# Layer 0's FFN: two groups of a modulation's rows in one PSUM bank, turned once, and both streams' gates turned together

## The chip, the cores and the metric

The kernel runs on one core of one Trainium2 chip. The metric is device time in microseconds (us) of one execution. Engines are named as in the profile: PE is TensorE's matmul pipe and PEld its weight load, DVE is VectorE, ACT is ScalarE, POOL is GpSimd, and SPq is the queue on which SyncE issues DMAs. L252 is line 252 of the kernel before.

## What is computed

Two transformer layers over 512 latent rows and 256 context rows (the two *streams*), 1024 columns wide. Every sub-layer is normed, scaled, shifted and gated by vectors that come from a conditioning vector of its stream:

```python
s_c = jax.nn.silu(c)
s_cc = jax.nn.silu(c_ctx)[None, :]
for l in range(DEPTH):
    mx = (s_c @ mod_w[l] + mod_b[l])[:, None, :]
    mc = (s_cc @ mod_w[l] + mod_b[l])[:, None, :]
    shx1, scx1, gx1, shx2, scx2, gx2 = jnp.split(mx, 6, axis=-1)
    shc1, scc1, gc1, shc2, scc2, gc2 = jnp.split(mc, 6, axis=-1)
    hx = _rms(x, norm_mix_w[l]) * (1.0 + scx1) + shx1
    ...
    x = x + gx1 * ax
    x = x + gx2 * _swiglu(_rms(x, norm_ffn_w[l]) * (1.0 + scx2) + shx2, ffn_w_in[l], ffn_w_out[l])
```

So a layer has six *modulations* (parts 0 to 5), each a product of a vector with 1024 rows by 1024 columns of `mod_w`. Parts 2 and 5 are the gates. Layer 1's parts 2 to 5 are needed for the latent stream alone.

## The kernel before

The work is written out in one order: layer 0's attention with its projections (to about 340 us in the profile), layer 0's FFN in two stages, gate/up products (about 428 to 764 us) and the way out (764 to 950 us), then layer 1 in the same manner. From early in layer 0's attention on, PE runs its instructions in the order in which the code is written (a manual schedule for PE). For DVE, ACT, POOL and the DMA queues a scheduler that works with modelled times picks the order, so a small edit can reorder them at some distance.

The gate/up stage is a list of matmul blocks (`product`, L933) for 22 slices f of the hidden width. Its operands come in as 128x512 pieces (`wr`), are split by ACT into a high part (`wbh`, L901) and by DVE or POOL into a low part (`wbl`, L911); ACT and DVE also add up the partial products (L938 to L973). In the list of blocks a hook stands twice per f from f = 2 on, 40 times in all. Each call of the hook makes one step of a stream of modulation work (`mod_stream`), so that the vectors that are needed later are made in the shade of the FFN's matmuls.

`mod_stream` takes a list of *groups* of 256-column *chunks*. A chunk is loaded as two pieces of 128 x 4 x 256 (L211). `products` multiplies them by the conditioning vectors and adds the eight row blocks, on DVE (L224, L226) for one stream and on ACT and POOL (L230 to L236) for the other; what is left is one accumulator `ma` of 128 x 256 per chunk and stream whose 128 rows are still to be summed. When all chunks of a group are through, `sums` runs, in two steps of the hook:

- step one: for each of the group's four accumulators one matmul with 32 columns of ones (L245) writes the column sums, 32 times over, into one quarter (32 partitions) of a PSUM tile `modrow`, and ACT copies it back to SBUF (L248);
- step two: two matmuls (L252) with a selection matrix from the constants turn these rows into columns, `modcol`, in the same PSUM bank, and DVE adds the bias, a chunk at a time (`add_mod`, L276), into `modc`; for parts 1 and 4 it also makes the scale `aff` (L280).

In the gate/up stage the groups are (layer, part) = (0, 5), (1, 0), (1, 1), for both streams, with two chunks in a group and so two groups for each of the three, and (1, 2) for the latent stream alone, with four chunks in one group: seven groups. All of them use the PSUM bank `acc1`, which nothing else uses there. In the way out three more groups follow, parts 3, 4 and 5 of layer 1, one stream and four chunks each.

A gate is multiplied with rows of tokens, so it is needed as a row on all partitions. `gate_mem` (L285) turns one stream's gate from 128 x 8 to 8 x 128 with one matmul (L288), copies it out of PSUM (L290, tile `grow`, two buffers) and stores it to DRAM (L292, `gmem`); `gate_row` (L294) later reads it back to all 128 partitions (L300, tile `g`, 512 KB). It is called twice at the end of the second head group of layer 0's attention (L1326), and through a list `gates` by the three hooks that follow the stream's end; `gate_mem(1, 5, 0)` comes in layer 1.

Transposes use two PSUM banks, `tr0` and `tr1`. `tr_tile` (L102) hands them out by turns, unless the caller names one. The attention of layer 0 names them for `ppt`, the transposed probabilities: even blocks go to `tr0` and are copied out by ACT (L617), odd blocks to `tr1` and are copied out by DVE (L615). The transposes of q and k (`qpt`, L535, and `kpt`, L543, copied out by ACT at L537 and L544) and a gate's (`gps`) take the banks by turns.

The way out (`way_out0`, L1001) makes two passes over f, three row tiles each, with PSUM sums in six banks. For each f it loads 512 KB of `ffn_w_out` (`wdr`, L1016) and the hidden rows (`hidm`, L1014), splits both (L998 on ACT, L999 on DVE) and issues 18 matmuls (L1030 to L1032). Its first act is to read the two gates (0, 5) back; they are first used at the end of the first pass (L471). It keeps the last two f of a pass back to finish bank by bank.

Of the kernel before, what the change touches and what calls it, by code (L numbers as in the profile page):

```python
# [19 lines left out]
P = 128  # L20
# [19 lines left out]

C_ID, C_S2, C_ONE, C_S4 = 0, 128, 130, 258
C_N = C_S4 + 12

# [20 lines left out]
def backbone(es: ExitStack, tc: tile.TileContext, x, c, ctx, c_ctx, mod_w, mod_b, norm_mix_w, norm_ffn_w,  # L64
# [133 lines left out]
    def mod_stream(groups, pool, bank):  # L198

        width = 256  # L200
        pieces = [(g, c, pc) for g in groups for c in g for pc in range(2)]
        accs, raws, full, rows = {}, [], [], []

# [36 lines left out]
        def sums(g):  # L240
            every = [acc for c in g for acc in accs.pop(c)]
            m = len(every)
            ps = bank_tile("modrow", [P, width])
            for j, acc in enumerate(every):
                nc.tensor.matmul(ps[32 * j:32 * j + 32, :], cst[:, C_ONE:C_ONE + 32], acc, start=True, stop=True,  # L245
                                 tile_position=(0, 32 * j))
            r = every[-1]
            nc.scalar.copy(r[:32 * m], ps[:32 * m])  # L248
            yield
            ps = bank_tile("modcol", [P, 2, m])  # L250
            for b in range(2):
                nc.tensor.matmul(ps[:, b, :], r[:32 * m, b * P:(b + 1) * P], cst[:32 * m, C_S4:C_S4 + m],  # L252
                                 start=True, stop=True)
            i = 0
            for l, part, n, streams in g:
                add_mod(l, part, 2 * n, 2 * n + 2, ps[:, :, i:i + streams], streams)
                i += streams

        while pieces or raws or full or rows:
            if rows:  # L260
                for _ in rows.pop():
                    pass
            if full:
                rows.append(sums(full.pop()))
                next(rows[0])
# [18 lines left out]

    def gate_mem(l, part, i, bank=None):  # L285

        ps = tr_tile("gps", [KT, P]) if bank is None else p_1.tile([KT, P], F32, name="gps", tag=bank)
        nc.tensor.transpose(ps, modc[l][:, part, :, i], ident)  # L288
        row = small.tile([KT, P], F32, name="grow", tag="grow", bufs=2)
        nc.vector.tensor_copy(row, ps)  # L290
        mem = gmem[l, part, i] = dram.tile([KT, P], F32, name="gmem", tag=f"gmem{l}{part}{i}")
        nc.sync.dma_start(mem, row)  # L292

    def gate_row(l, part, i, pool):  # L294

        if (l, part, i) not in gmem:
            gate_mem(l, part, i)
        g = pool.tile([P, D], F32, name=f"g{i}", tag=f"g{i}")
        with tc.issue_after(turn["load"].ins):
            nc.sync.dma_start(g, dram_rows(gmem[l, part, i].rearrange("k p -> (k p)")))  # L300
        return g
# [988 lines left out]
    if True:  # L1290
        for i, (b, t) in enumerate(steps):
# [11 lines left out]
            if b < 3:  # L1303
# [188 lines left out]

    gates = [(0, 5, 0), (0, 5, 1), (1, 2, 0)]

# [114 lines left out]
    if True:  # L1609
# [34 lines left out]
        xs0, xs1 = xs, [None] * NTX  # L1644
        gate_mem(1, 5, 0)
        o_t = [keep.tile([P, D], F32, name=f"o{t}", tag="xo", bufs=6) for t in range(NTX)]
# [230 lines left out]
def _constants():  # L1877
# [53 lines left out]
```

## Time and profile before

| what | value |
|---|---|
| runs | 1691.99, 1696.72, 1697.31 us; median 1696.72 us |
| span of the profiled execution | 1695.6 us, 1.1 us below the median of the runs |
| PE busy over the span | 1631.5 us (96%) |
| DVE, ACT, POOL busy | 1146.7, 937.0, 696.4 us |
| gate/up stage of layer 0 | 428 to 763.6 us |
| matmuls of `modrow` (L245) and `modcol` (L252), all ten groups | 80 and 40 records, two for each matmul of the code |
| matmuls of `gps` (L288) | 6 |

The profile is one execution. Busy times overlap between engines. A timeline row gives the start in the span, the length from the first start to the last end of the merged instructions, how many there are, and, in brackets, how long the engine stood idle just before and what ended that. Matmuls overlap with the next one, so what one costs is read from start to start and not from its length. A windows row gives the busy time of each engine in a stretch, the clock that PE was granted, the share of the time that the DMA engines were busy, and GB/s.

### The profile page before, as it was taken

What the parts mean: (1) busy time and instruction counts of PE and PEld (TensorE: products, weight loads), DVE (VectorE), ACT (ScalarE), POOL (GpSimd) and SP (SyncE); (2) the same over time, 40 slices, a digit from 0 to 9 for tenths busy, and PEclk for the clock granted to TensorE, in tenths of its full rate; (3) what the DMA queues carried; (4) which work ended last, traced back from release to release, by engine and by line L of the source; (5) the groups of instructions that cost most, each with busy time, mean ns of one, the idle gap of its engine ahead of it and who ended that gap; (6) DMA issues with size and microseconds to landing.
All of it is one profiled execution on the core that took longest, in us unless ns stands there. A gap on an engine that the chain in (4) does not pass through costs nothing. (4 is left out here: it accounts for less than half of the span.)

```text
span 1695.6 us, 28585 instructions
## 1 busy us (share of the span) xinstructions
PE 1631.5 (96%) x10390; PEld 1468.6 (87%) x10390; DVE 1146.7 (68%) x2014; ACT 937.0 (55%) x2011; POOL 696.4 (41%) x867
## 2 busy tenths in 40 slices
PE   6999999899999999999999989999999999999998
PEld 3977787677999999998777889999988899999887
DVE  3765656754799887767767656666666598887434
ACT  5565555745456665545554456666666555555320
POOL 2665554321346554412413366666664242221000
PEclk8999999999999999999999999999999999999999
DMA  9222221411455555439966311111112433331431
GB/s 319 69 71 74 70 70 50 164 60 38 129 167 172 164 159 162 134 108 347 296 184 189 99 43 38 48 42 44 50 45 97 125 93 102 111 101 57 137 99 62
DMA packets 218108, 194.64 MB, mean 115 GB/s; under 512 B 20016, under 2 KB 202864, under 8 KB 217968
## 3 DMA queue, kind: packets, MB, share of 16 engines
q1 hardware_dynamic: 217616, 192.62, 36.8%
q8 instruction: 81, 1.33, 0.3%
q14 instruction: 59, 0.48, 0.1%
q10 hardware_dynamic: 352, 0.21, 0.0%
HBM read 179.92 MB, written 12.87 MB: 114 GB/s over the span
## 5 line engine op out<-in xcount | busy, mean ns | idle before, releaser
L901 ACT CAST wbh<-wr 128x512 fp32r<-128x512 f32 x170 | 104.9, 621 | 130.2 <-PE p L933 73.4
L933 PE MATMUL p<-hT,wbh 128*128 128x256 f32 (+1 forms) x752 | 154.5, 299 | 0.0
L465 PE MATMUL inps<-wih,hT 128*128 128x384 f32 x512 | 144.2, 344 | 7.3 <-ACT qkv L677 7.3
L911 POOL TENSOR_TENSOR wbl<-wr,wbh 128x512 fp32r<-128x512 f32 x43 | 60.0, 1396 | 173.6 <-ACT wbh L901 173.6
L933 PEld LDWEIGHTS p<-hT,wbh 128*128 128x128 f32 x752 | 121.9, 191 | 0.2
L911 DVE TENSOR_TENSOR wbl<-wr,wbh 128x512 fp32r<-128x512 f32 x127 | 107.7, 858 | 21.0 <-ACT wbh L901 16.8
L933 PE MATMUL p<-hT,wbl 128*128 128x256 f32 (+1 forms) x376 | 111.9, 298 | 0.0
L933 PE MATMUL p<-t,wbh 128*128 128x384 f32 (+1 forms) x480 | 111.3, 318 | 0.0
L604 POOL TENSOR_SCALAR Pt<-Pt,rc 128x256 f32<-128x256 f32 (+3 forms) x96 | 74.6, 788 | 89.3 <-DVE rc L601 83.1
L231 POOL TENSOR_TENSOR modp<-modp 128x512 f32<-128x512 f32 x40 | 57.4, 1436 | 114.3 <-ACT modp L230 114.3
L465 PEld LDWEIGHTS inps<-wih,hT 128*128 128x128 f32 x512 | 93.3, 188 | 10.6 <-ACT qkv L677 9.7
L933 PE MATMUL p<-hTt,wbh 128*128 128x256 f32 (+1 forms) x480 | 101.0, 302 | 0.0
L887 POOL TENSOR_TENSOR wr<-wr 128x512 f32<-128x512 f32 x40 | 61.6, 1540 | 89.8 <-DVE ws L892 85.8
L933 PE MATMUL p<-b,wbh 128*128 128x384 f32 x368 | 93.8, 336 | 0.2 <-DVE c L961 0.2
L901 ACT CAST wbh<-ws 128x512 fp32r<-128x512 f32 x120 | 69.4, 579 | 43.1 <-PE p L933 29.0
L224 DVE SCALAR_TENSOR_TENSOR ma<-modw,cols,ma 128x256 f32<-128x256 f32 x140 | 89.2, 637 | 2.3
L592 ACT ACTIVATE Pt<-sc,nm 128x256 f32<-128x256 f32 (+3 forms) x96 | 67.6, 707 | 35.3 <-DVE nm L588 16.9
L465 PE MATMUL inps<-wil,hT 128*128 128x384 f32 x256 | 86.0, 336 | 0.0
L933 PEld LDWEIGHTS p<-t,wbh 128*128 128x128 f32 x480 | 82.9, 189 | 0.0
L911 DVE TENSOR_TENSOR wbl<-ws,wbh 128x512 fp32r<-128x512 f32 x120 | 81.7, 681 | 1.7 <-ACT wbh L901 1.6
L933 PEld LDWEIGHTS p<-hTt,wbh 128*128 128x128 f32 x480 | 78.3, 191 | 3.1 <-ACT modp L230 1.6
L230 ACT ACTIVATE modp<-modw,cols 128x256 f32<-128x256 f32 x160 | 68.4, 500 | 18.0 <-POOL ma L236 10.1
(355 smaller groups left out, 5217.9 us busy)
## 6 DMA issues: line engine op xcount, KB each, us to landing
modw<-in_mod_w_dram SPq DMA_DIRECT2D x96, 512.0 KB, 5.2
wr<-in_ffn_w_in_dram SPq DMA_DIRECT2D x176, 256.0 KB, 2.9
wdr<-in_ffn_w_out_dram SPq DMA_DIRECT2D x66, 512.0 KB, 3.7
wir<-in_od_w_in_dram SPq DMA_DIRECT2D x96, 128.0 KB, 2.3
hidm<-hid SPq DMA_DIRECT2D x44, 192.0 KB, 1.9
hr<-hidm SPq DMA_DIRECT2D x22, 192.0 KB, 3.5
x<-in_x_dram SPq DMA_DIRECT2D x8, 512.0 KB, 3.5
wir<-in_ev_w_in_dram SPq DMA_DIRECT2D x16, 256.0 KB, 3.5
```

Of the source, the lines that this page charges most:

```text
L224: nc.vector.scalar_tensor_tensor(acc, w[:, k], scale[k], acc, ALU.mult, ALU.add)
L230: nc.scalar.activation(pr[:, k], w[:, k], AF.Copy, scale=scale[k])
L231: nc.gpsimd.tensor_add(pr[:, 0:2], pr[:, 0:2], pr[:, 2:4])
L465: nc.tensor.matmul(ps, hs[j][:, k, :], ws[k // 2][z][:, k % 2, c0:c1], start=(k, j, z) == (0, 0, 0), stop=(k, j, z) == (KT - 1, 1, 0))
L592: turn["exp"] = nc.scalar.activation(p[:, :n], s, AF.Exp, bias=nm[:, c1], accum_out=sm[:, c1])
L604: nc.gpsimd.tensor_scalar(p[:, :n], p[:, :n], rc[:, hh:hh + 1], 1.0, ALU.mult, ALU.mult)
L887: nc.gpsimd.tensor_sub(w, raw[f, "G1"], w)
L901: nc.scalar.copy(hi, w)
L911: (nc.gpsimd if name == "G2" else nc.vector).tensor_sub(lo, raw[need[n]], f32(hi))
L933: nc.tensor.matmul(ps, w[:, k, :], H[b][h][:, k, :], start=first and k == 0 and q == 0, stop=final and k == 3 and q == 2, skip_group_check ...
```

## The change

For a modulation of both streams the two groups now share one `modrow` tile. The first group's four matmuls start the sums with a stationary matrix of 16 columns of ones and 16 of zeros; the second group's four add to the same bank with 16 of zeros and 16 of ones. So each quarter of the bank holds two rows' sums, 16 times each. Only after the second group ACT copies the bank, and two matmuls turn all eight rows at once, with a selection matrix of eight columns; DVE then adds the bias for all eight column blocks of both streams in one operation. Groups of one stream use ones throughout as before, and their four chunks also get one bias operation instead of four. `modcol` is now 128 x 8 x streams, and the matmul for each half of a chunk writes every second column block of it.

`gate_mem` takes the number of streams: with two it turns both gates in one matmul of 16 columns, copies 16 rows and stores them with one DMA, interleaved by column block. Read back, one stream's gate is then eight pieces of 512 bytes in DRAM, where it was one run of 4 KB. `grow` has one buffer. The constants have 48 more columns.

```diff
-C_ID, C_S2, C_ONE, C_S4 = 0, 128, 130, 258
-C_N = C_S4 + 12
+C_ID, C_S2, C_ONE, C_S4, C_S8 = 0, 128, 146, 290, 298
+C_N = C_S8 + 20
...
-            m = len(every)
-            ps = bank_tile("modrow", [P, width])
+            l, part, n, streams = g[0]
+            ends = 2 * (n + len(g)) == KT
+            if not n:
+                rowed.append(bank_tile("modrow", [P, width]))
+            ps = rowed[0]
+            one = C_ONE if not n and ends else C_ONE + P - 16 if not n else C_ONE - 16
             for j, acc in enumerate(every):
-                nc.tensor.matmul(ps[32 * j:32 * j + 32, :], cst[:, C_ONE:C_ONE + 32], acc, start=True, stop=True,
+                nc.tensor.matmul(ps[32 * j:32 * j + 32, :], cst[:, one:one + 32], acc, start=not n, stop=ends,
                                  tile_position=(0, 32 * j))
+            if not ends:
+                return
             r = every[-1]
-            nc.scalar.copy(r[:32 * m], ps[:32 * m])
+            nc.scalar.copy(r, rowed.pop())
             yield
-            ps = bank_tile("modcol", [P, 2, m])
+            ps = bank_tile("modcol", [P, KT, streams])
             for b in range(2):
-                nc.tensor.matmul(ps[:, b, :], r[:32 * m, b * P:(b + 1) * P], cst[:32 * m, C_S4:C_S4 + m],
+                nc.tensor.matmul(ps[:, b::2, :], r[:, b * P:(b + 1) * P], cst[:, C_S4:C_S4 + 4 * streams],
                                  start=True, stop=True)
-            i = 0
-            for l, part, n, streams in g:
-                add_mod(l, part, 2 * n, 2 * n + 2, ps[:, :, i:i + streams], streams)
-                i += streams
+            add_mod(l, part, 0, KT, ps, streams)
...
-    def gate_mem(l, part, i, bank=None):
+    def gate_mem(l, part, streams, bank=None):
...
-        nc.tensor.transpose(ps, modc[l][:, part, :, i], ident)
-        row = small.tile([KT, P], F32, name="grow", tag="grow", bufs=2)
+        nc.tensor.transpose(ps, cs, ident)
+        row = small.tile([2 * KT, P], F32, name="grow", tag="grow", bufs=1)[:KT * streams]
         nc.vector.tensor_copy(row, ps)
-        mem = gmem[l, part, i] = dram.tile([KT, P], F32, name="gmem", tag=f"gmem{l}{part}{i}")
-        nc.sync.dma_start(mem, row)
+        mem = dram.tile([KT, streams, P], F32, name="gmem", tag=f"gmem{l}{part}")
+        gmem.update({(l, part, i): mem[:, i, :] for i in range(streams)})
+        nc.sync.dma_start(mem.rearrange("k i p -> (k i) p"), row)
...
-            nc.sync.dma_start(g, dram_rows(gmem[l, part, i].rearrange("k p -> (k p)")))
+            nc.sync.dma_start(g.rearrange("p (k c) -> p k c", c=P), dram_rows(gmem[l, part, i]))
...
-                    for k in range(2):
-                        gate_mem(0, 2, k)
+                    gate_mem(0, 2, 2)
...
-    gates = [(0, 5, 0), (0, 5, 1), (1, 2, 0)]
+    gates = [(0, 5, 2), (1, 2, 1)]
...
-    k[:, C_S4:C_S4 + 4] = p[:, None] == 32 * np.arange(4)
+    k[:, C_S4:C_S4 + 8] = p[:, None] == 32 * (np.arange(8) % 4) + 16 * (np.arange(8) // 4)
```

How the order of instructions moves is shown at three places. The first is PE in the gate/up stage, one hook after the first group of (0, 5). `p` are the blocks' sums, `t`, `hT` and `wbh`, `wbl` their operands. Before:

```order
L933 MATMUL p_5741<-t_4884,wbh 128x384
L933 MATMUL p_5741<-t_4883,wbl 128x384
L252 MATMUL modcol<-cst,ma 128x4 x2
L933 MATMUL p_5929<-hT_110,wbh 128x384
L933 MATMUL p_5929<-hT_111,wbh 128x384
```

With the change, at the same place:

```order
L939 MATMUL p_5735<-t_4878,wbh 128x384
L939 MATMUL p_5735<-t_4877,wbl 128x384
L939 MATMUL p_5917<-hT_110,wbh 128x384
L939 MATMUL p_5917<-hT_111,wbh 128x384
L939 MATMUL p_5917<-hT_110,wbl 128x384
```

The pair of turning matmuls is gone here, and at two more such places; after the second group of each modulation it stands as `128x4x2 x2`. The rest of PE's order in the stage is the same, and so is the place of every `modrow`.

The second place is DVE in the same stage, one hook after the second group of (1, 1). `cg`, `c` are FFN partial sums. Before:

```order
L961 TENSOR_TENSOR c_7722<-p_7568,s_7600 128x384
L276 TENSOR_TENSOR modc_107<-modcol,bcol 128x4 x2
L911 TENSOR_TENSOR wbl<-ws,wbh 128x512
L280 SCALAR_TENSOR_TENSOR aff_109<-modc_107,cols 128x4 x2
L892 TENSOR_TENSOR ws<-wr 128x512
```

With the change:

```order
L967 TENSOR_TENSOR c_7691<-p_7538,s_7570 128x384
L279 TENSOR_TENSOR modc_107<-modcol,bcol 128x16
L917 TENSOR_TENSOR wbl<-ws,wbh 128x512
L283 SCALAR_TENSOR_TENSOR aff_109<-modc_107,cols 128x16
L898 TENSOR_TENSOR ws<-wr 128x512
```

Two small operations become one wider one, and at the first group of a modulation none is left. Over the whole kernel DVE issues 29 operations fewer, ACT 3, PE 8, and SPq 2.

The third place is PE in layer 0's attention, where the gates (0, 2) are turned. `sc` are scores, `mod` the attention's own modulation work. Before:

```order
L182 MATMUL mod<-modw,s_pad 32x256 x8
L191 MATMUL modcol<-cst,modr 128x2 x2
L288 MATMUL gps<-cst,modc_106 8x128 x2
L578 MATMUL sc<-kT,qt 128x256 x2
L612 MATMUL ppt<-cst,Pt 128x128 x8
```

With the change:

```order
L182 MATMUL mod<-modw,s_pad 32x256 x8
L191 MATMUL modcol<-cst,modr 128x2 x2
L293 MATMUL gps<-cst,modc_106 16x128
L584 MATMUL sc<-kT,qt 128x256 x2
L618 MATMUL ppt<-cst,Pt 128x128 x8
```

One `gps` instead of two takes one transpose bank instead of two. From here to the end of layer 0's attention `qpt` takes `tr0` and `kpt` takes `tr1`, where it was the other way round; ACT's and DVE's orders differ in some places of this stretch, mostly by one or two positions.

More of the change, by code (lines that the diff above doesn't have):

```diff
@@ L201, in mod_stream @@
         pieces = [(g, c, pc) for g in groups for c in g for pc in range(2)]
-        accs, raws, full, rows = {}, [], [], []
+        accs, raws, full, rows, rowed = {}, [], [], [], []
         def bank_tile(name, shape):
@@ L264, in mod_stream @@
                 rows.append(sums(full.pop()))
-                next(rows[0])
+                next(rows[0], None)
             if len(raws) == 2 or not pieces and raws:
@@ L1644, in backbone @@
         xs0, xs1 = xs, [None] * NTX
-        gate_mem(1, 5, 0)
+        gate_mem(1, 5, 1)
         o_t = [keep.tile([P, D], F32, name=f"o{t}", tag="xo", bufs=6) for t in range(NTX)]
```

7 lines of the change are left out of this document (5 added, 2 removed).

## The prediction

> **What bounds the kernel now.** I read the page first, then busy time by stretch for the places that the change touches.
>
> ```profile
> span 1695.6 us, 28585 instructions
> PE 1631.5 (96%) x10390; PEld 1468.6 (87%) x10390; DVE 1146.7 (68%) x2014; ACT 937.0 (55%) x2011; POOL 696.4 (41%) x867
> ...
> GB/s 319 69 71 74 70 70 50 164 60 38 129 167 172 164 159 162 134 108 347 296 184 189 99 43 38 48 42 44 50 45 97 125 93 102 111 101 57 137 99 62
> ```
>
> PE is busy for 96% of the span. By stretch (layer 0's attention after the gates are turned; one stretch inside it; then the gate/up stage; then the first pass of the way out and its end):
>
> ```profile
> core 0: us, PE busy (x) PEld busy (x) DVE busy (x) ACT busy (x) POOL busy (x), PEclk, DMA share, GB/s
> 221.00:335.00 114.00, 105.57 (x782) 83.05 (x782) 72.82 (x134) 71.95 (x160) 49.95 (x69) 1.00 0.31 104
> 310.00:315.00 5.00, 4.45 (x44) 3.52 (x43) 2.25 (x5) 3.15 (x6) 0.55 (x1) 1.00 0.99 375
> ...
> 500.00:550.00 50.00, 50.00 (x300) 48.67 (x298) 47.65 (x78) 29.57 (x64) 29.29 (x25) 1.00 0.60 180
> 700.00:750.00 50.00, 50.00 (x295) 49.16 (x294) 30.54 (x52) 25.67 (x48) 14.96 (x12) 1.00 0.24 72
> 765.00:840.00 75.00, 75.00 (x339) 61.60 (x338) 59.12 (x85) 42.29 (x77) 29.60 (x24) 1.00 0.99 327
> 840.00:850.00 10.00, 8.33 (x36) 6.32 (x35) 3.70 (x4) 5.04 (x8) 2.27 (x3) 0.99 0.79 266
> ```
>
> In the gate/up stage PE has no gap: 50.00 of 50 us at full clock. DVE is next with 47.65 of 50, but nothing on PE waits for it. So in this stage a matmul taken out of PE's order shortens the span by its slot, and operations taken from DVE and ACT bring nothing. In the attention PE stands idle for 114 - 105.57 = 8.4 us, so order and waits matter there. The way out's first pass is full on two sides: PE 75.00 of 75, DMA 0.99.
>
> **The turns that go.** PE's timeline at one of them:
>
> ```profile
> 549.08 0.51 PE L933 MATMUL p<-t,wbh 128*128 128x384 f32 x2
> 549.42 0.34 PE L933 MATMUL p<-t,wbl 128*128 128x384 f32 x1
> 549.60 0.50 PE L252 MATMUL modcol<-cst,ma 128*128 128x4 f32 x4
> 549.96 0.59 PE L933 MATMUL p<-hT,wbh 128*128 128x384 f32 x2
> 550.39 0.34 PE L933 MATMUL p<-hT,wbl 128*128 128x384 f32 x1
> ```
>
> From wbl to the next start are 549.60 - 549.42 = 0.18 us. Without the turn the next wbl would start where a block's third matmul does, 0.34 us after 549.60 (549.08 to 549.42); it starts at 550.39. The turn holds PE for 0.79 - 0.34 = 0.45 us. Three go: **-1.3 us**. The sums (`modrow`) keep their count, shape and place; adding to a bank instead of starting it is assumed to cost nothing, as the FFN's own blocks do it throughout.
>
> The wait behind: the second group's sums now need no released bank, since the first left it open, and nothing else uses `acc1`. ACT's copy and the turn come one hook apart, as before. On the other engines go three ACT copies and, in the stage, 15 small DVE operations:
>
> ```profile
> L276 DVE TENSOR_TENSOR modc<-modcol,bcol x48: 142/152/163, 14.0 to 939.4; 128x4 f32<-128x4 f32 x32, 128x2 f32<-128x2 f32 x16
> ```
>
> At 0.15 us that is 2.3 us of DVE, under PE's cover: zero.
>
> **The gates.** One gate's turn in the stage:
>
> ```profile
> 737.39 0.34 PE L933 MATMUL p<-b,wbl 128*128 128x384 f32 x1
> 737.57 0.27 PE L288 MATMUL gps<-cst,modc 128*8 128x128 f32 x1
> 737.60 0.61 PE L933 MATMUL p<-hTt,wbh 128*128 128x384 f32 x2
> 738.04 0.34 PE L933 MATMUL p<-hTt,wbl 128*128 128x384 f32 x1
> ```
>
> 738.04 - 737.57 - 0.34 = 0.13 us; one of three goes: **-0.1 us**. Sixteen stationary columns should load like eight. With one buffer for `grow`, the second gate's copy waits for the first row's store, but the hooks are several us apart: zero.
>
> **The attention after the gates.** One `gps` goes there too, and with it a bank turn, so `qpt` and `kpt` swap banks against `ppt`'s fixed ones. The places where PE's waits hang on that:
>
> ```profile
> 221.64 1.07 PE L612 MATMUL ppt<-cst,Pt 128*128 128x128 f32 x8 [0.31 <-DVE grow L290]
> ...
> 225.23 0.63 PE L612 MATMUL ppt<-cst,Pt 128*128 128x128 f32 x4
> 226.60 0.66 PE L612 MATMUL ppt<-cst,Pt 128*128 128x128 f32 x4 [0.73 <-ACT qt L537]
> ...
> 267.28 1.09 PE L612 MATMUL ppt<-cst,Pt 128*128 128x128 f32 x8 [0.69 <-ACT kT L544]
> ...
> 292.12 0.66 PE L612 MATMUL ppt<-cst,Pt 128*128 128x128 f32 x4 [0.21 <-ACT qt L537]
> ...
> 295.06 1.09 PE L612 MATMUL ppt<-cst,Pt 128*128 128x128 f32 x8 [0.46 <-ACT kT L544]
> ```
>
> Before, `qpt` was in `tr1`, so the first four `ppt` ran and the second four waited for ACT's copy of q. Swapped, the first four wait too, and the second four follow them: about one half block, 0.4 us, later at 225 and at 292. Where `kpt` was in `tr0` (267, 295) it is the reverse, some 0.4 us earlier. These four cancel. The wait for `grow` at 221.64 can go, since the one `gps` now sits in `tr1`, and a `gps` slot goes (0.1): between 0 and -0.4 us, and I take **-0.2**. If all five waits went, it would be -(0.31 + 0.73 + 0.69 + 0.21 + 0.46) = -2.4 us. The other bound is +3, from the longest wait of `ppt` on a copy of q in the half of the attention before, which DVE's and ACT's new order could bring here as well:
>
> ```profile
> PE ppt L612 <- ACT qt L537: 3.1, 2, 2.9
> ```
>
> **The gates' way back.** Each read of a two-stream gate becomes 8 x 128 pieces of 512 bytes instead of 128 of 4 KB. The nearest rows are loads in pieces of 512 bytes (`wr`) and of 4 KB (`wdr`), and the gates' own:
>
> ```profile
> wr<-in_ffn_w_in_dram SPq DMA_DIRECT2D x176, 256.0 KB, 2.9
> wdr<-in_ffn_w_out_dram SPq DMA_DIRECT2D x66, 512.0 KB, 3.7
> ...
> g<-gmem SPq DMA_DIRECT2D x6, 512.0 KB, 8.0
> ```
>
> By throughput: the DMA engines move 180 / 0.60 = 300 GB/s of full share at 500 to 550 us, where the loads are `wr` and 1 KB pieces, and 375 / 0.99 = 379 at 310 to 315, where they are mostly 4 KB. 512 KB (0.524 MB) take 1.75 and 1.38 us, so two gates cost 0.7 us more. In the attention (reads at 312, first use at 341) that has cover. In the way out the reads stand in the queue at 765 us, in front of loads that keep the DMA engines at 0.99, and the pass ends on such loads:
>
> ```profile
> 765.35 0.90 SPq L300 DMA_DIRECT2D g<-gmem  x2
> ...
> 843.21 1.05 ACT L998 CAST hT<-wdr 128x1024 fp32r<-128x1024 f32 x1 [4.14 <-DMA wdr<-in_ffn_w_out_dram]
> ...
> 847.96 0.50 PE L1030 MATMUL dps<-hT,hTt 128*128 128x512 f32 x1 [0.61 <-ACT hT L998]
> ...
> 849.53 0.60 PE L1031 MATMUL dps<-hT,hTt 128*128 128x512 f32 x1 [1.06 <-DVE hT L999]
> ```
>
> PE loses 1.67 us there to loads that come late, so up to 0.7 can pass through; bounds 0 and +0.7, and I take **+0.4**, the middle. The Trainium skill, "DMA: Bandwidth & Descriptors", section Specifications, puts the least transfer for line rate at 512 bytes; by that rule this term would be zero and the sum 0.4 lower. The 300 against 379 GB/s above speak for a small cost.
>
> **The rest.** The constants are 48 x 512 bytes = 25 KB longer at a start that loads at 319 GB/s: **+0.1**. Two stores of 4 KB become one of 8 KB, twice: zero.
>
> Sum: -1.3 - 0.1 - 0.2 + 0.4 + 0.1 = -1.1 us, a span of 1694.5. The profiled span lies 1.1 us below the median of the runs, 1696.72, so the time is **1695.6 us**, 0.07% less. A measurement of this kernel can tell about 0.3% from no change, that is 5.1 us: the runs before themselves lie 5.3 us apart.
>
> **The rivals.**
> *Given back at the pass's end.* If the first pass hangs on its loads alone, PE comes to them earlier and waits longer, and only the attention's share and the start are left: 1696.6. For it speak the 0.99 and the 4.14 us wait on `wdr`; against it, that the loads start when PE frees their places, so they move ahead with PE.
> *Strided sums.* `modcol` is now written with gaps: for two streams eight bytes, for one stream four, then as many left out. No row of before shows a matmul that writes so. If it doubled a turn's slot of 0.45, seven turns remain (three and one in the stage, three in the way out): +3.2, 1698.8. Against it: a turn writes four or eight columns. The Trainium skill, "PSUM — Partial Sum Buffer", section Specifications (TRN2), says that a non-contiguous access pattern slows matmuls significantly, by cachelines of 8 bytes; this rival is what it would do here.
> *Slower: the gate reads hold up the way out.* If the small pieces cost by number and a gate took 16 us instead of 8.0, both would push 16 us of queue before the loads of a pass that has 0.75 us of free DMA time until 840 and 2.1 in the last 10 us. PE would wait some 13 us longer at the end: about 1708.5. It decides from 9 us of added queue time on. Against it: `wr` lands 256 KB of such pieces in 2.9 us.
> *Much faster: the attention's new order.* If ACT's and DVE's changed order took away half of PE's 8.4 idle us there, -4.2 with the -1.4 of the stage: 1691.1. For it: ACT's copies of `ppt` move ahead of other work; against it: PE's order is fixed and four of the five waits only change places.
> That the turns don't go is no rival, since the order shows them gone.
>
> **How the numbers follow.** The forecast 0.60; given back 0.15; strided sums 0.10; held-up way out 0.07; the attention's order 0.08. The last is the only one below 1691.6 (faster by over 0.3%), the one before it the only one above 1701.8, so faster 0.08, same 0.85, slower 0.07. The range, 1691.5 to 1699.0, takes in the first three cases, the attention's lower bound of -2.4 and most of its upper one.
>
> **What would show it.** Right: the `modcol` matmuls of the stage and the way out are 28 records instead of 40 at about 0.25 us, and a turn still holds PE for 0.45; the first way-out matmul starts 1.4 us earlier against the stage's start, with PE still at 50.00 of 50; ACT's copies of `modrow` are seven; PE's idle time from 221 to 335 us is 8.4 within 2; at the first pass's end PE waits 1.7 to 2.4 us. Wrong: longer `modcol` records (strided sums), gates that land after 12 us or more and a longer wait at the first pass's end (held up), or idle time in the attention that moves by over 3 us. A gap of PE inside the gate/up stage would undo the first term.

## The result and the profile after

The changed kernel takes 1699.37 us (median of 11 runs, 1695.48 to 1704.98), the kernel before beside it 1696.21 us (11 runs). The ratio is 1.0024, 95% interval 1.0015 to 1.0034: slower by some 4 us, where 1.1 us less was forecast and the range ended at 1699.0. The profiled execution of the changed kernel is the slowest of its eleven, 1704.98 us, so the spans are compared place by place, not as wholes. Of its page:

```profile
span 1703.2 us, 28521 instructions
PE 1641.3 (96%) x10376; PEld 1476.8 (87%) x10376; DVE 1148.5 (67%) x1985; ACT 935.9 (55%) x2008; POOL 698.7 (41%) x867
```

PE has 14 matmul records fewer (10390 before) and is busy 9.8 us longer (1631.5 before). First what the change was made of. One turn in the gate/up stage, in PE's timeline, and the records of the turns and of ACT's copies by tile:

```profile
552.32 0.34 PE L939 MATMUL p<-t,wbl 128*128 128x384 f32 x1
552.49 0.51 PE L258 MATMUL modcol<-cst,ma 128*128 128x8 f32 x4
552.85 0.60 PE L939 MATMUL p<-hT,wbh 128*128 128x384 f32 x2
553.29 0.34 PE L939 MATMUL p<-hT,wbl 128*128 128x384 f32 x1
```

```profile
L258 PE MATMUL modcol<-cst,ma x28: 167/253/257, 552.5 to 945.3; 128*128 128x4 f32 x16, 128*128 128x8 f32 x12
```

```profile
L254 ACT COPY ma<-modrow x7: 364/372/373, 544.2 to 941.5; 128x256 f32<-128x256 f32 x7
```

A turn holds PE for 553.29 - 552.49 - 0.34 = 0.46 us, there are 28 records and seven copies: all as forecast, and writing with gaps costs nothing here (median 253 ns, as before). Now the places, by busy time in stretches (layer 0's attention, the gate/up stage, the first pass of the way out, its end):

```profile
221.00:335.00 114.00, 105.58 (x801) 83.32 (x799) 72.12 (x134) 71.29 (x160) 52.94 (x71) 1.00 0.32 105
765.00:840.00 75.00, 74.71 (x339) 61.70 (x339) 56.41 (x82) 39.47 (x71) 26.05 (x22) 1.00 0.97 320
840.00:850.00 10.00, 10.00 (x46) 8.29 (x45) 5.08 (x6) 4.22 (x9) 4.47 (x4) 1.00 0.94 317
850.00:860.00 10.00, 6.89 (x17) 4.36 (x16) 6.22 (x7) 5.45 (x10) 2.78 (x2) 0.69 0.63 183
860.00:870.00 10.00, 9.80 (x42) 7.69 (x42) 8.16 (x12) 6.06 (x8) 1.79 (x5) 0.96 0.63 202
427.00:763.00 336.00, 336.00 (x1947) 330.40 (x1946) 277.13 (x426) 185.50 (x367) 150.77 (x117) 1.00 0.49 148
```

PE has no gap in the gate/up stage, 336.00 of 336. At the pass's end it stands idle for 3.1 us of 10, and the granted clock is 0.69 there. In the profile of before the clock is below full at this place too, but for less time:

```profile
850.00:860.00 10.00, 10.00 (x39) 8.16 (x38) 8.75 (x12) 5.14 (x7) 2.58 (x3) 0.84 0.77 232
```

Start by start against before, the profiled execution is 2.6 us behind when the stage begins (the start, where the granted clock differs from execution to execution: two later profiles of kernels with the same constants come to the stage 5 us earlier), 3.9 at its end, 6.4 after the pass's end and 7.5 from layer 1's FFN on.

The stage is the place where the forecast had its gain. Its first matmul and the last one on `pz`, before:

```profile
427.42 0.34 PE L933 MATMUL p<-hT 128*128 128x384 f32 x1
...
756.75 0.34 PE L933 MATMUL pz<-hT,wbl 128*128 128x384 f32 x1
```

and after:

```profile
430.05 0.34 PE L939 MATMUL p<-hT 128*128 128x384 f32 x1
...
760.21 0.34 PE L939 MATMUL pz<-hT,wbl 128*128 128x384 f32 x1
```

329.33 us became 330.16, though three turns are gone. (Between this matmul and the first of the way out stands a wait for DVE of 0.1 to 1.0 us that differs from execution to execution; without it this length agrees to 0.2 us between kernels below that have the same matmuls and the same addresses.) The groups of matmuls in the stage show where it went; the number behind the bar is the busy time of the whole group. Before:

```profile
L933 PE MATMUL p<-b,wbh 128*128 128x384 f32 x368 | 93.8, 336 | 0.2 <-DVE c L961 0.2
L933 PE MATMUL p<-t,wbh 128*128 128x384 f32 x320 | 81.7, 336 | 0.0
...
L933 PE MATMUL pz<-hT,wbh 128*128 128x384 f32 x160 | 40.8, 336 | 0.0
L933 PE MATMUL p<-hT,wbl 128*128 128x384 f32 x104 | 34.9, 336 | 0.0
```

after:

```profile
L939 PE MATMUL p<-b,wbh 128*128 128x384 f32 x368 | 94.8, 339 | 0.5 <-DVE c L967 0.5
L939 PE MATMUL p<-t,wbh 128*128 128x384 f32 x320 | 81.3, 335 | 0.0
...
L939 PE MATMUL pz<-hT,wbh 128*128 128x384 f32 x160 | 41.1, 338 | 0.0
L939 PE MATMUL p<-hT,wbl 128*128 128x384 f32 x104 | 35.2, 338 | 0.0
```

The same matmuls, the same number, full clock, and no wait up to the last one on `pz` (the 0.2 and 0.5 us on DVE stand behind it), but those on `b` and `hT` are 2 to 3 ns longer, and those on `t` 1 ns shorter. From start to start a matmul of `b` on `wbh` takes 0.1767 us instead of 0.1742; summed over all 1,872 matmuls of the stage, the faster ones on `t` counted against it, the difference is some 2 us. Nothing in the change touches these instructions. What it does touch is where their operands lie. The traces have no addresses; these and all below are those of the built programs. The constants are 192 bytes longer in each partition, so all tiles behind them lie 192 bytes higher (`hT`, `hTt`), and `grow` has 512 bytes less, so the phases' pools lie 320 bytes lower (`b`, the modulation's tiles, in layer 1 the ring of weights). `t` and layer 0's ring of weights are laid out from the other end of SBUF and do not move.

SyncE's queue behind the gates' reads, before:

```profile
766.34 1.76 SPq L211 DMA_DIRECT2D modw<-in_mod_w_dram  x3
```

After, with ACT and PE at the first pass's end:

```profile
769.23 1.14 SPq L306 DMA_DIRECT2D g<-gmem  x2
770.46 4.04 SPq L211 DMA_DIRECT2D modw<-in_mod_w_dram  x3
```

```profile
849.46 1.05 ACT L1004 CAST hT<-wdr 128x1024 fp32r<-128x1024 f32 x1 [4.38 <-DMA wdr<-in_ffn_w_out_dram]
...
851.83 0.50 PE L1037 MATMUL dps<-hT,hTt 128*128 128x512 f32 x1 [0.76 <-DVE hT L1005]
```

The three loads behind the gates' reads take 4.04 us to issue instead of 1.76. The wait on `wdr` is 4.38 us, before 4.14. The gates themselves land no later (median 7.0 us, before 8.0).

So there were four theories: **1**, the addresses slow the stage; **2**, the reads in pieces of 512 bytes lengthen the pass's end; **3**, the bank that stays open between two groups slows the stage; **4**, chance of the profiled execution.

### The profile page after: what moved, and what is told of

The parts are those of the page before. It is cut to its first block, busy times and chain, and to the rows that moved or that the text cites. A ratio compares the mean times of both kernels' runs of the same rounds, so it can differ in the third digit from the quotient of the medians.

```text
span 1703.2 us, 28521 instructions
## 1 busy us (share of the span) xinstructions
PE 1641.3 (96%) x10376; PEld 1476.8 (87%) x10376; DVE 1148.5 (67%) x1985; ACT 935.9 (55%) x2008; POOL 698.7 (41%) x867
## 5 line engine op out<-in xcount | busy, mean ns | idle before, releaser
L471 PEld LDWEIGHTS inps<-wih,hT 128*128 128x128 f32 x512 | 93.8, 188 | 9.9 <-ACT qkv L683 9.1
L939 PE MATMUL p<-b,wbh 128*128 128x384 f32 x368 | 94.8, 339 | 0.5 <-DVE c L967 0.5
L939 PEld LDWEIGHTS p<-t,wbh 128*128 128x128 f32 x480 | 82.9, 189 | 0.0
L471 PE MATMUL inps<-wihi,hT 128*128 128x384 f32 x256 | 77.3, 359 | 2.1 <-DVE modc L279 1.9
```

Of the source, the lines that this page charges most:

```text
L471: nc.tensor.matmul(ps, hs[j][:, k, :], ws[k // 2][z][:, k % 2, c0:c1], start=(k, j, z) == (0, 0, 0), stop=(k, j, z) == (KT - 1, 1, 0))
L939: nc.tensor.matmul(ps, w[:, k, :], H[b][h][:, k, :], start=first and k == 0 and q == 0, stop=final and k == 3 and q == 2, skip_group_check ...
```

## Experiments

None of the kernels leaves out work. "Stage" is the length from the first matmul to the last on `pz`, as above; where the expectations speak of the stage, it runs to the first matmul of the way out, the wait included (336.2 us before, 337.4 after).

### Addresses and pieces, each undone

`a1_addr_back` is the changed kernel with the addresses of before: the pattern of 16 ones and 16 zeros moves out of the constants into a tile that takes the place of `grow`'s second buffer.

```diff
-C_ID, C_S2, C_ONE, C_S4, C_S8 = 0, 128, 146, 290, 298
-C_N = C_S8 + 20
+C_ID, C_S2, C_ONE, C_S4 = 0, 128, 130, 258
+C_N = C_S4 + 12
...
+    ends16 = small.tile([P, P], F32, name="ends16", tag="ends16", bufs=1)
+    nc.gpsimd.memset(ends16, 0.0)
+    nc.gpsimd.memset(ends16[:, 16:32], 1.0)
```

> The changed kernel with the SBUF addresses of the kernel before: the constants are 270 columns again, and the second buffer of grow's size holds the pattern of ones and zeros. Theory 1 (the new addresses make each matmul of the gate/up stage about 1% longer while the modulation runs): the stage, 1.2 us longer than before in the changed kernel, becomes 1.3 us shorter than before, and the time falls by 2.5 us against the changed kernel; the first pass's end keeps its longer wait. Theory 2 (the gate reads in pieces of 512 bytes hold up the first pass of the way out): no change to either, the time stays 3 us above before. Theory 3 (the pairing itself slows the stage, through the bank that stays open between two groups): the stage stays 1.2 us longer than before at the old addresses too. Theory 4 (only the start and the granted clock differ from run to run): the stage's length differs between profiles of the same kernel by as much as 1 us.

`a2_gates_whole` is the changed kernel with its own addresses and the gates one after the other in DRAM:

```diff
-        mem = dram.tile([KT, streams, P], F32, name="gmem", tag=f"gmem{l}{part}")
-        gmem.update({(l, part, i): mem[:, i, :] for i in range(streams)})
-        nc.sync.dma_start(mem.rearrange("k i p -> (k i) p"), row)
+        mem = dram.tile([streams, KT, P], F32, name="gmem", tag=f"gmem{l}{part}")
+        gmem.update({(l, part, i): mem[i] for i in range(streams)})
+        for i in range(streams):
+            nc.sync.dma_start(mem[i], row[i::streams])
```

> The changed kernel with the gates of two streams stored one after the other in DRAM, by two DMAs, so that each is read back in runs of 4 KB as before; addresses as in the changed kernel. Theory 2 (reads in pieces of 512 bytes hold up the way out): issue of the three loads behind the reads in SyncE's queue falls from 4.0 us to about 1.8, PE's loss at the first pass's end falls by 1 to 2.5 us to what it was before, and the time falls by as much against the changed kernel. Theory 1 (addresses) and theory 3 (the open bank): the gate/up stage stays 1.2 us longer than before, the time falls by less than 1 us. Theory 4: the first pass's end differs between profiles by 1 us or more whatever the gates do.

`a3_both` has both edits.

> The changed kernel with both: the addresses of the kernel before, and gates that are read in runs of 4 KB. If theories 1 and 2 hold together, what is left of the change is its gain: the stage 1.3 us shorter than before, the end of the first pass as before, the time 1 to 2 us below the kernel before. If only one of them holds, 1 to 2 us above it; under theory 3 (the open bank) the stage stays 1.2 us longer.

`b1_addr_shift` is the other way round: the kernel before, with nothing of the change but its addresses.

```diff
-C_N = C_S4 + 12
+C_N = C_S4 + 60
...
-        row = small.tile([KT, P], F32, name="grow", tag="grow", bufs=2)
+        if i == 0:
+            grown[0] = small.tile([32 + KT, P], F32, name="grow", tag="grow", bufs=1)
+        row = grown[0][32 * i:32 * i + KT]
```

> The kernel before with the SBUF addresses of the changed kernel: 48 more unused columns of constants, and the two gates' rows in one tile of one buffer. Nothing else of the change is in it. Theory 1 (addresses): the gate/up stage is 2.6 us longer than in the kernel before, its start-to-start times of matmuls on b and wbh go from 0.174 to about 0.177 us, and the time rises by 2.5 us. Theories 2, 3 and 4: stage and time as before, within 1 us.

| kernel | median us | ratio to before, interval | stage us |
|---|---|---|---|
| before | 1694.85 | 1 | 329.33 |
| a1, addresses of before | 1693.64 | 0.9999 (0.9990 to 1.0007) | 327.79 |
| a2, gates in 4 KB | 1695.80 | 1.0008 (0.9998 to 1.0018) | 330.09 |
| a3, both | 1691.53 | 0.9979 (0.9968 to 0.9990) | 327.79 |
| b1, before at the new addresses | 1700.07 | 1.0037 (1.0024 to 1.0051) | 331.54 |

The stage's ends in b1 and its groups:

```profile
424.94 0.33 PE L935 MATMUL p<-hT 128*128 128x384 f32 x1
...
756.48 0.34 PE L935 MATMUL pz<-hT,wbl 128*128 128x384 f32 x1
```

```profile
L935 PE MATMUL p<-b,wbh 128*128 128x384 f32 x368 | 94.8, 338 | 0.6 <-DVE c L963 0.6
L935 PE MATMUL p<-t,wbh 128*128 128x384 f32 x320 | 81.3, 335 | 0.0
...
L935 PE MATMUL pz<-hT,wbh 128*128 128x384 f32 x160 | 41.1, 338 | 0.0
L935 PE MATMUL p<-hT,wbl 128*128 128x384 f32 x104 | 35.1, 338 | 0.0
```

These are the groups of the changed kernel, out of the kernel before: with the addresses alone `b` goes from 93.8 to 94.8. And the changed kernel at the old addresses, a3:

```profile
425.54 0.34 PE L940 MATMUL p<-hT 128*128 128x384 f32 x1
...
753.33 0.34 PE L940 MATMUL pz<-hT,wbl 128*128 128x384 f32 x1
```

has a stage of 327.79 us, 1.54 below before: the forecast of 3 x 0.45 for the turns and 0.13 for the gate's turn. Theory 1 holds. Theory 3 falls, since the open bank is in a1 and a3 too. Theory 4 falls for the stage: a1 and a3 agree to 0.01 us, the changed kernel and a2 to 0.07. The addresses cost more than the stage's 2.2 to 2.4 us: 0.37% in the kernel before, 0.25% (1.0024 against 0.9999) and 0.29% (1.0008 against 0.9979) in the changed one. Some of the rest is in layer 1's projections, whose 512 matmuls of `wih` on `hT` go from 144.2 to 145.1 us in b1; the others were not followed up. Before, and in b1:

```profile
L465 PE MATMUL inps<-wih,hT 128*128 128x384 f32 x512 | 144.2, 344 | 7.3 <-ACT qkv L677 7.3
```

```profile
L467 PE MATMUL inps<-wih,hT 128*128 128x384 f32 x512 | 145.1, 345 | 6.2 <-ACT qkv L679 6.2
```

Theory 2 stays unclear here: a3 is 0.2% faster than a1, but a1's profile, with the same pieces, has no longer wait at the pass's end than before.

### Half of the shift

> The kernel before with half of the shift of addresses: only the pools behind the small tiles lie 320 bytes lower per partition (b, and the modulation's modw, ma and modp among them); the constants, hT and hTt stay. Nothing else is changed. Two versions of the address theory: (1a) the place of PE's own moving operand counts: then only the matmuls on b slow down (0.1742 to 0.1767 us, 1.6 us in sum for both parts), those on hT and hTt keep their 0.1742 to 0.1797 us. (1b) the place of the modulation's tiles counts, which other engines and DMA write and read at the same time: then all operands slow down, also hT and hTt, and t, whose address is the same in all kernels, becomes 0.001 us faster; the stage is 2.6 us longer than before.

> The kernel before with the other half of the shift: only the constants and what lies behind them up to the small tiles (hT, hTt among them) lie 192 bytes higher per partition; b and the modulation's tiles stay. (1a) PE's own moving operand counts: only the matmuls on hT and hTt slow down (about 1 us in sum), those on b stay at 0.1742 us. (1b) the modulation's tiles count: nothing slows down, the stage is as long as before within 0.3 us.

Both are the kernel before with `grow` in one tile; d2 has

```diff
+            grown[0] = small.tile([32 + KT, 176], F32, name="grow", tag="grow", bufs=1)
+        row = grown[0][32 * i:32 * i + KT, :P]
```

and d3 the same with 208 columns, and `C_N = C_S4 + 60`. d2 took 1692.71 us, 0.9983 (0.9968 to 0.9998); d3 1689.16 us, 0.9962 (0.9945 to 0.9979). In the stage both are slower than before, 330.15 and 330.21 us, and (1a) is right: d2's groups on `b` alone are longer, d3's on `hT` alone:

```profile
L935 PE MATMUL p<-b,wbh 128*128 128x384 f32 x368 | 94.7, 338 | 0.2 <-DVE c L963 0.2
...
L935 PE MATMUL p<-hT,wbl 128*128 128x384 f32 x104 | 34.9, 336 | 0.0
```

```profile
L935 PE MATMUL p<-b,wbh 128*128 128x384 f32 x368 | 93.7, 335 | 0.2 <-DVE c L963 0.2
...
L935 PE MATMUL p<-hT,wbl 128*128 128x384 f32 x104 | 35.1, 338 | 0.0
```

Neither theory expected that each half alone makes the whole kernel faster, while both together make it slower. The gain is in layer 1's gate/up stage, taken from its first matmul to the first of layer 1's way out: 225.65 us before (1345.15 to 1570.80), 222.20 in d2, 215.85 in d3. There `hT` lies in the part that d3 moves, and the ring of weights in the part that d2 moves; with both moved, by 192 up and 320 down, their distance changes by 512 bytes and the stage is as before. That points to a distance and not to a place: theory **R**, the distance between a matmul's moving operand and the weights that are loaded beside it. Theory **A**, the place itself, is its rival.

### Distance or place

`e1_ring1_pad` is the kernel before with one line more:

```diff
     ring = Pool("ring1")
+    ring.pool.tile([P, 80], F32, name="pad", tag="pad", bufs=1)
```

> The kernel before with 320 unused bytes ahead of layer 1's ring of weights, so that in layer 1's FFN the weights (wbh, wbl) lie 64 bytes above the moving operands hT and hTt modulo 512, where they lay 256 above; nothing else moves up to there. In the run with only hT and the constants shifted the same distance came about from the other side, and layer 1's matmuls on hT and hTt went from 0.120 to 0.113-0.115 us. Theory R (the distance modulo 512 between a matmul's moving operand and the weights loaded beside it sets its pace): the same here, layer 1's gate/up stage 9 to 10 us shorter than before, the time 0.5% below before; layer 0's stage 336.2 us as before. Theory A (the place of the moving operand itself counts): hT has not moved, so layer 1's stage stays as before.

`r1_relative` is b1 with such a line for layer 0, in the pool of `t`, so that the ring moves and `t` doesn't.

```diff
     blkt = Pool("blkt0", "right")
+    blkt.pool.tile([P, 80], F32, name="pad", tag="pad", bufs=1)
```

> The kernel before with the addresses of the changed kernel, and layer 0's ring of weights moved 320 bytes down as well (320 is 192 the other way modulo 512), so that the distance of wbh and wbl from b, hT and hTt is what it was in the kernel before, and only t is now at another distance. Theory R: the matmuls on b, hT and hTt go back from 0.1766, 0.1763 and 0.1760 to 0.1742 us, the stage is within 0.7 us of before's 336.2. Theory A: they stay slow, the stage stays 2.6 us longer than before. Layer 1's attention, whose weights are not moved, keeps its loss under both.

e1 took 1685.13 us, 0.9955 (0.9940 to 0.9971). In layer 1's stage, PE's matmuls in 100 us and one group, before:

```profile
1400.00:1500.00 100.00, 100.00 (x835) 100.00 (x834) 86.61 (x129) 56.24 (x110) 25.87 (x20) 1.00 0.37 106
```

```profile
L933 PE MATMUL p<-hTt,wbh 128*128 128x256 f32 x320 | 59.3, 283 | 0.0
```

and in e1:

```profile
1400.00:1500.00 100.00, 100.00 (x877) 100.00 (x876) 90.10 (x136) 58.68 (x115) 26.39 (x21) 1.00 0.39 112
```

```profile
L933 PE MATMUL p<-hTt,wbh 128*128 128x256 f32 x320 | 56.4, 276 | 0.0
```

835 matmuls became 877 in the same time, PE at 100% both times; from start to start 0.1133 us instead of 0.1200. `hT` had not moved. The stage fell from 225.65 to 216.26 us, and layer 0's stayed at 329.33. r1 took 1697.09 us, 1.0016 (1.0007 to 1.0025), where b1 had 1.0037; its stage is 329.40 us, and the groups are back or on the way:

```profile
L935 PE MATMUL p<-b,wbh 128*128 128x384 f32 x368 | 94.2, 337 | 0.2 <-DVE c L963 0.2
...
L935 PE MATMUL p<-hT,wbl 128*128 128x384 f32 x104 | 34.9, 336 | 0.0
```

Theory R holds in both layers, A falls. The place of the weights alone falls as well: in b1 layer 0's ring had not moved, and in d3 layer 1's had not. `b` on `wbh` (94.2, before 93.8, in b1 94.8) comes back by a little over half. `inps`, which has no operand in the ring that moved, stays at 145.1 us, as both theories expected.

`m0_map` makes the distances many: 64 bytes of room behind each of the ring's buffers.

```diff
-                    ring.tile([P, 4, P], F32R, name=name, tag=name, bufs=ahead) for name in ("wbh", "wbl"))
+                    ring.tile([P, 4 * P + (16 if l == 0 else 0)], F32R, name=name, tag=name, bufs=ahead)[:, :4 * P]
+                    .rearrange("p (k c) -> p k c", c=P) for name in ("wbh", "wbl"))
```

> The kernel before with 64 bytes of room behind each of the six buffers of wbh and of wbl in layer 0's ring, so that each buffer lies 64 bytes further modulo 512 than the one before it. Theory R: the matmuls of one moving operand no longer have one pace; they fall into groups by the buffer of their weights, from 0.173 to 0.177 us or more, and the groups depend on the distance alone. Theory A: one pace for each moving operand, as before.

One run, 1695.27 us. Each matmul's time to the next start (those with a wait left out), by the address of its weights less that of its moving operand, modulo 512; 170 to 270 matmuls a column:

```
distance   64     320    192    448    0      256    128    384
mean us    0.1735 0.1734 0.1745 0.1747 0.1750 0.1750 0.1757 0.1760
```

Distances that differ by 256 agree to 0.3 ns, so among the multiples of 64 that occur here the period is 256 bytes; 64 is best and 128 worst. Modulo 256, the kernel before has 64 for `b`, `hT` and `hTt`, and the changed one 128: by this table the change took them from the best distance to the worst. `t` is at 0 in both.

The expectation that the distance alone decides is not met. The scatter inside a column is larger than between the columns: the distance explains 8% of the variance. In the same trace the distance from the moving operand to the *next* matmul's weights counts about as much (sorted by it, the means run from 0.1734 us at 192 to 0.1755 at 128), and both distances together explain 17%. The neighbours count for `t` too. Its own distance is 0 before and after and 192 in r1; from the seventh matmul of a block on it takes 0.1733 us in all three, as little as the best column above, and all that it gains in the changed kernel lies in the first six (0.1758 us before, 0.1737 after), behind a block with another operand. So the table ranks the distances of one trace and is no price list, and the rest of the scatter stays open.

In layer 1 the distance of `hT` and `hTt` is 0 before and after (0.1200 us), 192 in d2 (0.118) and 64 in d3 and e1 (0.1133 for `hTt`, 0.114 for `hT`).

### The gates' pieces

`c1_pieces512` is the kernel before with the interleaved store and the read in pieces alone, `c2_pieces128` the same with pieces of 128 bytes:

```diff
-            nc.sync.dma_start(g, dram_rows(gmem[l, part, i].rearrange("k p -> (k p)")))
+            nc.sync.dma_start(g.rearrange("p (k c) -> p k c", c=128), dram_rows(gmem[l, part, i]))
```

> The kernel before with one part of the change alone: the gates of two streams are stored interleaved, so that each is read back in 8 x 128 pieces of 512 bytes; turns, rows, stores and addresses as before. Theory 2 (the pieces hold up the queue): the issue of the three loads behind the reads takes about 4 us instead of 1.8, the first pass's end comes 0.7 to 2.5 us later against the stage's end, and the time rises by 1 to 3 us. If what the changed kernel lost at the pass's end was chance: the issue is longer, pass's end and time within 0.5 us of before.

> The same with the suspected cost made larger: pieces of 128 bytes, 4096 for each gate. Theory 2: SyncE's queue is held up for far longer than 4 us, the loads behind it come late, and the first pass ends later by several us: at a guess four times the loss of the pieces of 512 bytes, so 3 to 10 us. If the reads were hidden, the time stays within 1 us.

c1: 1695.10 us, 1.0004 (0.9989 to 1.0019). c2: 1697.68 us, 1.0008 (0.9993 to 1.0022). The queue is held up as expected, in c1 for 4.21 us (a2, where the changed kernel reads in runs of 4 KB, has 1.63),

```profile
765.53 4.21 SPq L211 DMA_DIRECT2D modw<-in_mod_w_dram  x3
```

and yet, 450 matmuls into the way out, c1 is 1.4 us ahead of before. That doesn't clear the pieces, since the profile of before has a stretch at lower clock there and c1's has none. In c2 reads and loads take 7.65 us to issue, PE is 1.35 us behind before when it comes to the pass's end, and layer 0's way out is 0.4 us longer in all. That is far from four times anything, and the time (0.08%, 1.4 us) can't be told from no change. At the good addresses, e1's line in the changed kernel:

> The changed kernel at the addresses of the kernel before, with gates in runs of 4 KB, and with the 320 bytes ahead of layer 1's ring. Theory R: the gains add up, 1.3 us in layer 0's stage and 9 to 10 us in layer 1's; about 12 us below the kernel before. Theory A: as without the 320 bytes, 2 to 4 us below.

> The changed kernel at the good addresses (those of before, and 320 bytes ahead of layer 1's ring), but with the gates of two streams stored and read as the change has it, in pieces of 512 bytes. Where the reads cost 0.2% of the time (as between the changed kernel's two versions at the old addresses), this is 2 to 4 us slower than the same kernel with runs of 4 KB beside it. Where they cost what the kernel before lost to them alone (0.04%, interval -0.11 to 0.19%), within 1 us of it.

> The same with the gates in runs of 4 KB, as the other half of the pair: 12 to 13 us below the kernel before, as it was.

g1_best took 1681.25 us, 0.9923 (0.9909 to 0.9936), and again 1680.66, 0.9918 (0.9905 to 0.9932): the gains of the change (0.21% in a3) and of the distance in layer 1 (0.45% in e1) add up within their intervals. g2, with the pieces, took 1683.37 us, 0.9931 (0.9919 to 0.9944). Its pass's end, and g1_again's:

```profile
840.00:850.00 10.00, 7.47 (x26) 5.14 (x25) 4.94 (x5) 5.99 (x9) 1.38 (x2) 0.80 0.65 204
850.00:860.00 10.00, 10.00 (x39) 7.91 (x37) 8.86 (x14) 5.45 (x7) 2.46 (x3) 0.86 0.70 223
```

```profile
840.00:850.00 10.00, 9.68 (x43) 7.66 (x43) 6.50 (x9) 5.59 (x8) 3.14 (x2) 1.00 0.65 200
850.00:860.00 10.00, 8.48 (x35) 6.11 (x34) 7.54 (x11) 6.78 (x9) 1.48 (x4) 1.00 0.68 211
```

The three pairs that differ in the pieces alone (and in the store, one DMA for both gates or two) stand 0.16%, 0.20% and 0.13% apart, always to the pieces' cost: 2.2 to 3.4 us. The kernel before with them alone lost 0.04%, with an interval that holds 0.13 and 0.16. So the cost is about 2 us, more than the +0.4 of the sum, and not shown beyond doubt.

Where it falls is not shown. From the first matmul of the way out to the 360th after it, every kernel but c2 takes 82.9 to 83.1 us (c2 84.25), so up to the pass's end the pieces of 512 bytes delay nothing. To the 450th after it, behind the waits of the pass's end, the eleven profiles with runs of 4 KB take 106.1 to 109.0 us (before 107.9, g1_best 108.3, g1_again 106.3), and the four with pieces of 512 bytes 106.5, 107.3, 109.6 and 110.7. Two of the four lie above all the others, but executions with runs of 4 KB differ by 2.9 us among themselves, so one profile of a kernel can't price the pieces. A stretch at lower clock is part of these differences and no mark of the pieces: in the 10 us from 850 the clock is 0.69 in the changed kernel and 0.86 in g2, but also 0.84 in before and in r1 and 0.83 in b1, which read runs of 4 KB, and 1.00 in a1, c1 and c2. What decides that stays open.

## Why the prediction was wrong

**PE bounds the stage.** Right: 336.00 of 336 us, and a turn that goes is a slot that goes.

**The turns and the gate's turn.** Forecast -1.3 and -0.1, measured 329.33 - 327.79 = 1.54 us at equal addresses. The two assumptions, that adding to an open bank costs nothing and that 16 stationary columns load like eight, fit this sum: 3 x 0.45 and 0.13 make 1.48.

**The attention.** The mechanism was right in part, the size off. `ppt`'s waits after, in PE's timeline:

```profile
228.97 1.09 PE L618 MATMUL ppt<-cst,Pt 128*128 128x128 f32 x8 [0.91 <-ACT qt L543]
...
280.64 1.09 PE L618 MATMUL ppt<-cst,Pt 128*128 128x128 f32 x8 [0.29 <-ACT qt L543]
...
294.53 1.09 PE L618 MATMUL ppt<-cst,Pt 128*128 128x128 f32 x8 [0.68 <-ACT qt L543]
```

At 225 and 292 all eight now wait for q at once, where the second four did, and both waits on `kT` and the one on `grow` are gone. Matmul by matmul against before, a1, a2, a3 and the changed kernel agree to 0.3 us in each step: -0.6 where the gates are turned (the wait for `grow` and the slot); about 0 at 225 us, +1.0 for the first half and -0.9 with the second, which follows without a wait; -0.2 to -0.3 up to 262; -0.9 at `kT` at 267; +1.0 from 275 to 285, where waits for `modc` (0.20 us) and for q (0.29 at 280.64) stand that were not there before; -0.6 to -0.7 at q and `kT` from 285 to 300. From 207 to 327 us that makes 1.1 to 1.4 us, against 0.2 or less in the kernels that differ from before in addresses or pieces alone. I took -0.2. The places of q and `kT` don't cancel by halves as I thought, the turn of the gates brings more than its bound of -0.4, and the new waits at 275 to 285 I did not see.

**The rest: the step that failed.** "The constants are 48 x 512 bytes = 25 KB longer at a start that loads at 319 GB/s: +0.1", and the single buffer of `grow`: zero. I priced the bytes that are loaded and the wait that one buffer could bring, and not that both sizes move every tile behind them. By b1, that is +0.37% (0.24 to 0.51), 6 us; by the pairs in the changed kernel 0.25% and 0.29%, 4 to 5 us. It took all of the gain of 0.21% (a3; with the new addresses, a2, 1.0008), and no rival held it. In layer 0's stage the runs show by what: matmuls that wait for nothing get slower at the new distance between their two operands, 2.2 to 2.4 us of the stage. Where the rest of the 4 to 6 us falls is shown only in part.

**The gates' way back.** Taken as +0.4 with 0 to +0.7 for bounds; it is about 2 us by three pairs, out of these bounds, unsettled as told. I had bounded it by throughput alone, and left out the queue that is held up (4.04 instead of 1.76 us) and the clock, which is below full at the pass's end in the profile of before already (0.84). That the cost comes by either of them is not shown: c1 has the queue held up and no loss. By the rule of the Trainium skill, "DMA: Bandwidth & Descriptors", section Specifications, the term would have been zero; the three pairs speak against that, though c1 alone would agree with it.

**The rivals.** Strided sums: refuted, 253 ns. Given back at the pass's end: a3 speaks against it, with 0.21% or 3.6 us less (1.7 to 5.4 by its interval), where the attention's 1.2 would be all that is left. The slower rival named the place where the profile of the changed kernel waits longer (3.1 us, before 1.67), but by landing times that never came (7.0 us, it needed 16), and with 13 us as its price. The attention's new order, at 4.2 us: a third of it came.

In sum: -1.5 for the stage and -1.2 for the attention, +2 for the pieces and +4 to 6 for the addresses give some +3 to +5; measured +0.24%, 4.1 us.

## What to carry to other kernels

A tile that grows or shrinks moves every tile that is laid out behind it, and PE can feel it: before pricing a change, compare the two layouts, and when matmuls without any wait change their pace, look at the addresses of both operands before looking for a stall. Where PE is at 100%, a pad of some hundred bytes ahead of a ring of weights is among the cheapest experiments there are; here 320 bytes brought 0.45%, more than the whole change at its best (0.21%). An A/B test of an edit that also changes a size tests two things, so undo the layout by itself.

## What the runs showed of the hardware

The pace of back-to-back matmuls without waits, at full clock, depends on the distance between weights and moving operand modulo 256 bytes: 0.1133 us at 64, 0.118 at 192 and 0.1200 at 0 for 256 columns, a spread of 6%; on average 0.1734 at 64 to 0.1760 at 128 for 384 columns, 1.5%. The matmuls beside it in the order count as well (17% of the variance explained with the next one's weights, 8% without). The Trainium skill, "SBUF — State Buffer", section "A bandwidth-pool intuition that's wrong (but worth ruling out)", gives PE a second, independent read port for weight loads; by that alone no distance could matter, and the measurement decides. Which part of a matmul takes the longer time is not shown.

At the pass's end some executions have lower clock and some have not: 0.69 of full speed over the 10 us from 850 in the changed kernel and 0.96 over the next 10, which at half speed would be (0.31 + 0.04) x 10 / 0.5 = 7 us; 0.99 and 0.84 over the 10 us from 840 and from 850 in before, by the same working 3.4 us; 1.00 in d2. How long PE waits there does not decide it alone: 1.67 us in before, 2.61 in d2. The Trainium skill, "TensorE: Matmul & The Clock Gate", Part 1, has the clock at half or full in windows of about 3.4 us; two such windows fit the rows of the changed kernel and one those of before.
